# Values of a head and filling placed between the score steps of the wide attention heads

## The chip, the cores and the metric

The kernel runs on one core of a Trainium2 chip. A core has a matrix engine (TensorE, PE in the profile), VectorE (DVE), ScalarE (ACT), GpSimd (POOL) and SyncE (SP), which here only issues DMAs; they run side by side, each through its own list of instructions in order, and semaphores order them among one another. Matmuls read SBUF and write PSUM. The metric is the device time of one execution in microseconds, the median of three runs.

## The reference

One inference step of a decoder with two layers of width 1024, for a prompt of 1024 tokens and for 8 sample tokens, in f32. Layer 0 has four differential attention heads and four HGRN2 heads, layer 1 has eight forgetting-attention heads and four mLSTM heads. In each layer the heads' outputs go through an output projection with a residual, and then through a squared-ReLU MLP (1024 to 4096 to 1024) with a residual. The two kinds of attention at issue, cut to what matters:

```
# differential attention, per head: two causal softmaxes, one set of values (128 wide)
probs(q, k) = softmax(where(mask, q @ k.T * scale + bias, NEG))
o = (probs(q1, k1) - lam * probs(q2, k2)) @ v          # then an RMS norm per head

# forgetting attention, per head (64 wide)
s = q @ k.T * scale + fq[:, None] - fk[None, :]
o = softmax(where(mask, s, NEG)) @ v
```

## The kernel before

**Precision.** An f32 operand a is held as two parts, ah and al (a minus ah), both in a form that the matrix engine takes at full rate. A product then takes three matmuls: hi by hi, hi by lo, lo by hi. The parts of weights come from `wsplit` (L111 ff): a DMA brings 512 KB into wr (2 buffers), ScalarE copies them to wh (L117), GpSimd makes wl = wr - wh (L118).

**Stages.** The prompt is worked in two halves of 512 tokens, u = 0 and 1. The second half of attention is called wide, since its queries look back on up to 1024 keys: `diff_wide` (L746 ff, four heads, layer 0) and `fox_wide` (L1357 ff, eight heads, layer 1). A wide head has two groups, g = 2 and 3, each of two blocks of 128 queries. A query block has a score step: matmuls into S (L596 to L599; two PSUM buffers of 1024 columns), on VectorE a reduction for the row's extreme (L642, L644), on ScalarE the exponential e with its sum (L646), and then the scaling of e by the reciprocal sum (L769 to L772 in the differential heads, where a block has two score steps, m = 0 and 1; L1376 and L1380 in the forgetting heads). S is free again when its exponential is done.

Then a group is multiplied with the values in pairs of key blocks (3 pairs for g = 2, 4 for g = 3): `tr` transposes the probabilities of a pair on the matrix engine into pm (L664), ScalarE and VectorE split them into Ph and Pl (L652, L653), and `pv` multiplies them with the values' parts into po (L679). The values of a head are themselves transposed into pm and split: `diff_values` (transposes L702, Vh L704 on ScalarE, Vl L705 on VectorE) and `fox_values` (L1312, L1316, L1317; two heads in one pass, VV). pm is a single PSUM buffer, which these transposes share with those of the probabilities and with the sums of `head_norm` (hsq L294, hms L296, hrs L298 to L301, ho L303), the end of a differential head.

**Filling.** While a wide stage runs, the matrix engine is also given another half's output projection and MLP, the generator `half` (L1500 ff): parts of up to nine matmuls of 512 columns (L151), whose results VectorE adds to x (L1522), splits (xl L249, sq L261) or rectifies (L1495 to L1498). `tick(n)` adds n times a rate to a credit and takes parts from the generator until the credit is spent; a unit is 4096 columns, which is eight matmuls of 512. In both wide stages the rate is 1. What of the half is left when the stages end is drained without anything between.

**Order.** A tile scheduler sets the order of each engine's list from the program's order and its own timeline. In the wide stages the first matmul of every part of filling is tied (`issue_after`, L150) behind the last score, transpose or value product of the program so far, so that filling stays about where `tick` put it.

**The loop that the change touches** is `attend` (L602 ff). The groups of all heads form one list. A prologue prepares the first group, ticks 5, and does all its score steps, with tick(1.6) behind each. Then, group by group, a pair's transposes (`tr`), a tick and the next group's share of score steps, and the products (`pv`). A group marked late (only g = 2 in `diff_wide`) has its score steps held for the last two pairs of the group before. The values of head 0 are made inside `tr` of the first pair, so behind all score steps of the first group; those of later heads at the end of the head before's first group. `head_norm` of a differential head comes at the end of its group 3, next to the score steps of the next head.

Of the kernel before, what the change touches and what calls it, by code (L numbers as in the profile page):

```python
# [57 lines left out]
class Group:  # L58


    def __init__(self, prep, steps, pairs, tr, pv, end, late=False):
        self.prep, self.steps, self.pairs, self.tr, self.pv, self.end, self.late = prep, steps, pairs, tr, pv, end, late


class Step:
# [536 lines left out]
    def attend(self, groups, depth, lead, gap):  # L602

        self.chain = True
        N = len(groups)
        for G in groups[:depth + lead]:
            G.prep()
        self.tick(5)  # L610
        for G in groups[:depth]:
            for step in G.steps:
                step()
                self.tick(1.6)
        for n, G in enumerate(groups):
            if n + depth + lead < N:
                groups[n + depth + lead].prep()
            nxt = groups[n + depth] if n + depth < N else None
            todo = list(nxt.steps) if nxt else []
            for j in range(G.pairs):  # L620
                parts = G.tr(j)
                share = 0 if nxt and nxt.late and j < G.pairs - 2 else -(-len(todo) // (G.pairs - j if not (nxt and nxt.late) else min(2, G.pairs - j)))
                self.tick(max(gap - 0.4 * share, 0.4))
                for _ in range(share):
                    todo.pop(0)()
                G.pv(j, parts)
            G.end()
        self.chain = False
# [117 lines left out]
    def diff_wide(self, hd, pm, pS):  # L746
# [26 lines left out]
            P[h, i] = es[0]  # L773

        def tr(h, g, j):
            if h == j == 0 and g == 2:
                V[0] = self.diff_values(vt[0], u, hd, pm)
            if g == 2 and j == 0:
                po[h] = pm.tile([128, 512], F32, name="po", tag="po", bufs=1)
                if h < 3:  # L780
                    vt[h + 1] = self.values(self.O["va"][128 * h + 128:128 * h + 256, :], u, hd)
            return self.prob_t(hd, pm, (P[h, 2 * g], P[h, 2 * g + 1]), g, j)
# [16 lines left out]
        for h in range(4):  # L799
            for g in (2, 3):  # L800
                steps = [lambda h=h, i=i, m=m: score(h, i, m) for i in (2 * g, 2 * g + 1) for m in range(2)]
                groups.append(Group(lambda h=h, g=g: prep(h, g), steps, g + 1, lambda j, h=h, g=g: tr(h, g, j),
                                    lambda j, p, h=h, g=g: pv(h, g, j, p), lambda h=h, g=g: end(h, g), late=g == 2))
        self.attend(groups, 1, 0, 1.3)


# [550 lines left out]
    def fox_wide(self, hd, pm, pS):  # L1357
# [24 lines left out]

        def tr(h, g, j):
            i, r = divmod(h, 2)
            if h == j == 0 and g == 2:
                VV[0] = self.fox_values(vt[0], u, hd, pm)
            if g == 2 and j == 0:
                po[h] = pm.tile([128, 512], F32, name="po", tag="po", bufs=1)
                if r and i < 3:
                    vt[i + 1] = load(i + 1)  # L1390
            return self.prob_t(hd, pm, (P[h, 2 * g], P[h, 2 * g + 1]), g, j)
# [17 lines left out]
        for h in range(8):  # L1409
            for g in (2, 3):  # L1410
                groups.append(Group(lambda h=h, g=g: prep(h, g), [lambda h=h, qi=qi: score(h, qi) for qi in (2 * g, 2 * g + 1)], g + 1,
                                    lambda j, h=h, g=g: tr(h, g, j), lambda j, p, h=h, g=g: pv(h, g, j, p), lambda h=h, g=g: end(h, g)))
        self.attend(groups, 1, 1, 1.3)

    def fox_ones(self, W, hd):
# [489 lines left out]
```

## Time and profile before

| | |
|---|---|
| median of three runs | 2897.57 us (2889.6 to 2901.08) |
| the profiled execution | 2897.19 us |
| its span in the trace | 2895.4 us |
| mean granted clock of the matrix engine | 0.973 of full speed |
| PE busy | 2748.0 us, 95% |
| DVE / ACT / POOL busy | 48% / 36% / 39% |

The profile comes from one execution. "Busy" is time in which an instruction of the engine runs. The granted clock is the matrix engine's own, 1.00 at its full 2.4 GHz and 0.50 at its lower level of 1.2 GHz; a mean between the two is a mixture of both. A row of the timeline gives the start of an instruction from the span's start, its duration, the engine, the line of the kernel, what it writes and reads, how many are merged, and in brackets how long the engine had been idle and which instruction's end let it go on. Matmuls are pipelined: the distance of two starts, not the duration, is what one costs.

### The profile page before, as it was taken

What the parts mean: (1) busy time and instruction counts of PE and PEld (TensorE: products, weight loads), DVE (VectorE), ACT (ScalarE), POOL (GpSimd) and SP (SyncE); (2) the same over time, 40 slices, a digit from 0 to 9 for tenths busy, and PEclk for the clock granted to TensorE, in tenths of its full rate; (3) what the DMA queues carried; (4) which work ended last, traced back from release to release, by engine and by line L of the source; (5) the groups of instructions that cost most, each with busy time, mean ns of one, the idle gap of its engine ahead of it and who ended that gap; (6) DMA issues with size and microseconds to landing.
All of it is one profiled execution on the core that took longest, in us unless ns stands there. A gap on an engine that the chain in (4) does not pass through costs nothing. (4 is left out here: it accounts for less than half of the span.)

```text
span 2895.4 us, 44560 instructions
## 1 busy us (share of the span) xinstructions
PE 2748.0 (95%) x17404; PEld 2449.9 (85%) x17406; DVE 1377.6 (48%) x2666; ACT 1038.9 (36%) x1741; POOL 1142.3 (39%) x689
## 2 busy tenths in 40 slices
PE   8999997989989999999999989989999998999998
PEld 6999886777878878889999979968877776999997
DVE  5134378666664363474322255366544434523234
ACT  4111365552222232463232332155543222423233
POOL 2323323323764434423334435743323343344443
PEclk9999998999999999999999999999999998999999
DMA  4332454224545444423322244643235333322222
GB/s 143 107 125 75 152 163 127 89 83 154 159 115 164 132 163 147 154 88 104 121 95 88 91 158 147 222 128 93 77 110 163 110 107 126 110 89 95 90 94 74
DMA packets 174684, 349.72 MB, mean 121 GB/s; under 512 B 28914, under 2 KB 67298, under 8 KB 174474
## 3 DMA queue, kind: packets, MB, share of 16 engines
q1 hardware_dynamic: 174250, 346.81, 37.0%
q8 instruction: 137, 2.24, 0.3%
q0 software_dynamic: 224, 0.07, 0.2%
q14 instruction: 73, 0.60, 0.1%
HBM read 297.92 MB, written 48.88 MB: 120 GB/s over the span
## 5 line engine op out<-in xcount | busy, mean ns | idle before, releaser
L118 POOL TENSOR_TENSOR wl<-wr,wh 128x1024 fp32r<-128x1024 f32 (+1 forms) x361 | 866.2, 2400 | 1336.0 <-ACT wh L117 1293.1
L117 ACT ACTIVATE wh<-wr 128x1024 fp32r<-128x1024 f32 (+1 forms) x361 | 381.7, 1058 | 1088.1 <-PE acc L151 875.0
L151 PE MATMUL acc<-xh,wh 128*128 128x264 f32 (+2 forms) x2208 | 715.0, 325 | 18.1 <-DVE x L1522 8.0
L151 PE MATMUL acc<-xl,wh 128*128 128x264 f32 (+2 forms) x2208 | 711.3, 323 | 3.1 <-DVE xl L249 3.1
L151 PE MATMUL acc<-xh,wl 128*128 128x264 f32 (+2 forms) x2208 | 709.9, 322 | 0.0
L151 PE MATMUL acc<-uh,wh 128*128 128x512 f32 (+2 forms) x1856 | 607.4, 331 | 21.7 <-DVE x L1522 13.2
L151 PE MATMUL acc<-ul,wh 128*128 128x512 f32 (+2 forms) x1856 | 599.6, 324 | 6.9 <-DVE ul L1489 5.6
L151 PE MATMUL acc<-uh,wl 128*128 128x512 f32 (+2 forms) x1856 | 597.6, 323 | 0.0
L151 PEld LDWEIGHTS acc<-xh,wh 128*128 128x128 f32 x2208 | 420.3, 191 | 51.5 <-issue 10.5
L151 PEld LDWEIGHTS acc<-xl,wh 128*128 128x128 f32 x2208 | 420.7, 191 | 35.6 <-DVE xl L249 4.3
L151 PEld LDWEIGHTS acc<-xh,wl 128*128 128x128 f32 x2208 | 420.0, 190 | 29.4 <-issue 1.2
L1522 DVE TENSOR_TENSOR x<-acc,x 128x256 f32<-128x256 f32 (+1 forms) x464 | 238.3, 517 | 379.0 <-PE acc L151 376.9
L151 PEld LDWEIGHTS acc<-uh,wh 128*128 128x128 f32 x1856 | 353.0, 192 | 56.7 <-DVE x L1522 17.0
L151 PEld LDWEIGHTS acc<-ul,wh 128*128 128x128 f32 x1856 | 354.2, 191 | 33.6 <-DVE ul L1489 7.6
L151 PEld LDWEIGHTS acc<-uh,wl 128*128 128x128 f32 x1856 | 353.8, 191 | 26.8 <-issue 0.4
L1495 DVE SCALAR_TENSOR_TENSOR acc<-acc,rb 128x256 f32<-128x256 f32 (+2 forms) x192 | 100.2, 524 | 242.4 <-PE acc L151 237.7
L151 PE MATMUL acc<-ih,wh 128*128 128x512 f32 (+3 forms) x600 | 193.0, 322 | 7.3 <-ACT wh L117 4.7
L151 PE MATMUL acc<-ih,wl 128*128 128x512 f32 (+3 forms) x600 | 192.2, 323 | 6.5 <-POOL wl L118 6.5
L151 PE MATMUL acc<-il,wh 128*128 128x512 f32 (+3 forms) x600 | 192.2, 321 | 0.0
L225 DVE TENSOR_TENSOR z<-acc,rb 128x512 f32<-128x512 f32 (+2 forms) x138 | 69.6, 511 | 231.2 <-PE acc L151 216.6
L1498 DVE TENSOR_TENSOR ul<-acc,uh 128x256 fp32r<-128x256 f32 (+2 forms) x192 | 98.5, 513 | 135.6 <-ACT uh L1497 134.9
L151 PEld LDWEIGHTS acc<-ih,wh 128*128 128x128 f32 (+1 forms) x600 | 113.8, 190 | 16.8 <-ACT wh L117 6.7
(409 smaller groups left out, 3406.1 us busy)
## 6 DMA issues: line engine op xcount, KB each, us to landing
wr<-in_w_up SPq DMA_DIRECT2D x128, 512.0 KB
wr<-in_w_down SPq DMA_DIRECT2D x128, 512.0 KB
wr<-in_w_in_o SPq DMA_DIRECT2D x48, 512.0 KB
wr<-in_w_out SPq DMA_DIRECT2D x32, 512.0 KB
wr<-in_w_in_e SPq DMA_DIRECT2D x27, 512.0 KB
qd<-qS SPq DMA_DIRECT2D x64, 128.0 KB
dk<-in_cache_k_a SPq DMA_DIRECT2D x32, 256.0 KB
dk<-in_cache_v_a SPq DMA_DIRECT2D x32, 256.0 KB
```

The source lines that it names most:

```text
L117: nc.scalar.activation(h[:, :kk, :m], r[:, :kk, :m], AF.Copy)
L118: nc.gpsimd.tensor_tensor(l[:, :kk, :m], r[:, :kk, :m], raw(h[:, :kk, :m]), op=ALU.subtract)
L151: nc.tensor.matmul(out, lhsT=w[:, k, :m], rhs=a[:, sl], start=(n == 0), stop=(n == last))
L225: nc.vector.tensor_tensor(d, p, r, op=ALU.mult)
L1495: nc.vector.scalar_tensor_tensor(p, p, 0.0, self.rb[u][:, sl], op0=ALU.max, op1=ALU.mult)
L1498: nc.vector.tensor_tensor(L[:, sl], p, raw(H[:, sl]), op=ALU.subtract)
L1522: nc.vector.tensor_tensor(x[f][:, sl], pt[:, :m], x[f][:, sl], op=ALU.add)
```

## The change

Two things are moved; the instructions themselves stay the same, on every engine. `attend` calls a group's new function `values` behind the first score step of the prologue, and `tr` no longer does it. And where the next group is late, the tick ahead of a pair's score steps is not lowered for them, and a tick(1) stands between one score step and the next. That holds for heads 1 to 3 of `diff_wide`; no group of `fox_wide` is late.

```diff
--- before.py
+++ after.py
@@ -58,8 +58,8 @@
 class Group:
 
 
-    def __init__(self, prep, steps, pairs, tr, pv, end, late=False):
-        self.prep, self.steps, self.pairs, self.tr, self.pv, self.end, self.late = prep, steps, pairs, tr, pv, end, late
+    def __init__(self, prep, steps, pairs, tr, pv, end, late=False, values=None):
+        self.prep, self.steps, self.pairs, self.tr, self.pv, self.end, self.late, self.values = prep, steps, pairs, tr, pv, end, late, values
 
 
 class Step:
@@ -609,9 +609,11 @@
             G.prep()
         self.tick(5)
         for G in groups[:depth]:
-            for step in G.steps:
+            for n, step in enumerate(G.steps):
                 step()
                 self.tick(1.6)
+                if n == 0 and G is groups[0]:
+                    G.values()
         for n, G in enumerate(groups):
             if n + depth + lead < N:
                 groups[n + depth + lead].prep()
@@ -620,9 +622,12 @@
             for j in range(G.pairs):
                 parts = G.tr(j)
                 share = 0 if nxt and nxt.late and j < G.pairs - 2 else -(-len(todo) // (G.pairs - j if not (nxt and nxt.late) else min(2, G.pairs - j)))
-                self.tick(max(gap - 0.4 * share, 0.4))
-                for _ in range(share):
+                late = share and nxt.late
+                self.tick(gap if late else max(gap - 0.4 * share, 0.4))
+                for i in range(share):
                     todo.pop(0)()
+                    if late and i < share - 1:
+                        self.tick(1)
                 G.pv(j, parts)
             G.end()
         self.chain = False
@@ -773,8 +778,6 @@
             P[h, i] = es[0]
 
         def tr(h, g, j):
-            if h == j == 0 and g == 2:
-                V[0] = self.diff_values(vt[0], u, hd, pm)
             if g == 2 and j == 0:
                 po[h] = pm.tile([128, 512], F32, name="po", tag="po", bufs=1)
                 if h < 3:
@@ -800,7 +803,8 @@
             for g in (2, 3):
                 steps = [lambda h=h, i=i, m=m: score(h, i, m) for i in (2 * g, 2 * g + 1) for m in range(2)]
                 groups.append(Group(lambda h=h, g=g: prep(h, g), steps, g + 1, lambda j, h=h, g=g: tr(h, g, j),
-                                    lambda j, p, h=h, g=g: pv(h, g, j, p), lambda h=h, g=g: end(h, g), late=g == 2))
+                                    lambda j, p, h=h, g=g: pv(h, g, j, p), lambda h=h, g=g: end(h, g), late=g == 2,
+                                    values=lambda: V.update({0: self.diff_values(vt[0], u, hd, pm)})))
         self.attend(groups, 1, 0, 1.3)
 
 
@@ -1382,8 +1386,6 @@
 
         def tr(h, g, j):
             i, r = divmod(h, 2)
-            if h == j == 0 and g == 2:
-                VV[0] = self.fox_values(vt[0], u, hd, pm)
             if g == 2 and j == 0:
                 po[h] = pm.tile([128, 512], F32, name="po", tag="po", bufs=1)
                 if r and i < 3:
@@ -1409,7 +1411,8 @@
         for h in range(8):
             for g in (2, 3):
                 groups.append(Group(lambda h=h, g=g: prep(h, g), [lambda h=h, qi=qi: score(h, qi) for qi in (2 * g, 2 * g + 1)], g + 1,
-                                    lambda j, h=h, g=g: tr(h, g, j), lambda j, p, h=h, g=g: pv(h, g, j, p), lambda h=h, g=g: end(h, g)))
+                                    lambda j, h=h, g=g: tr(h, g, j), lambda j, p, h=h, g=g: pv(h, g, j, p), lambda h=h, g=g: end(h, g),
+                                    values=lambda: VV.update({0: self.fox_values(vt[0], u, hd, pm)})))
         self.attend(groups, 1, 1, 1.3)
 
     def fox_ones(self, W, hd):
```

The matrix engine's list at the start of `diff_wide`, before: K_4648 and K_4651 are the parts of the first map's keys, K_4661 and K_4664 those of the second map's; hms is the last norm of the stage before, vt the values of head 0.

```order
L296 MATMUL hms<-hsq,ones 128x512
L596 MATMUL S<-K_4648,Q_4647 128x512
L599 MATMUL S<-K_4651,Q_4647 128x512
L596 MATMUL S<-K_4648,Q_4647 128x128
L599 MATMUL S<-K_4651,Q_4647 128x128
L596 MATMUL S<-K_4661,Q_4660 128x512
L599 MATMUL S<-K_4664,Q_4660 128x512
L596 MATMUL S<-K_4661,Q_4660 128x128
L599 MATMUL S<-K_4664,Q_4660 128x128
L702 MATMUL pm<-ident,vt 128x128 x4
```

And with the change, from the same place on:

```order
L296 MATMUL hms<-hsq,ones 128x512
L596 MATMUL S<-K_4648,Q_4647 128x512
L599 MATMUL S<-K_4651,Q_4647 128x512
L596 MATMUL S<-K_4648,Q_4647 128x128
L599 MATMUL S<-K_4651,Q_4647 128x128
L707 MATMUL pm<-ident,vt 128x128 x4
L596 MATMUL S<-K_4661,Q_4660 128x512
L599 MATMUL S<-K_4664,Q_4660 128x512
L596 MATMUL S<-K_4661,Q_4660 128x128
L599 MATMUL S<-K_4664,Q_4660 128x128
L596 MATMUL S<-K_4648,Q_4647 128x512
```

The values' first four transposes stood behind two score steps and now stand behind one; the second four move ahead of the first two filling matmuls.

The matrix engine's list at the turn from head 0 to head 1 in `diff_wide`, before: K_5555 and K_5568 with their partners are head 1's keys, hms is head 0's norm, e its probabilities.

```order
L596 MATMUL S<-K_5555,Q_5554 128x128
L599 MATMUL S<-K_5558,Q_5554 128x128
L296 MATMUL hms<-hsq,ones 128x512
L596 MATMUL S<-K_5568,Q_5567 128x512
L599 MATMUL S<-K_5571,Q_5567 128x512
L596 MATMUL S<-K_5568,Q_5567 128x128
L599 MATMUL S<-K_5571,Q_5567 128x128
L596 MATMUL S<-K_5555,Q_5554 128x512
L599 MATMUL S<-K_5558,Q_5554 128x512
L596 MATMUL S<-K_5555,Q_5554 128x256
L599 MATMUL S<-K_5558,Q_5554 128x256
L664 MATMUL pm<-ident,e 128x128 x4
```

With the change (there K_5609 and K_5612 are the second map's keys of head 1), from the end of the filling inside the second score on; twelve more filling rows stand ahead of these, and three where lines are left out:

```order
L151 MATMUL acc<-ul,wh 128x512
L151 MATMUL acc<-uh,wl 128x512
L599 MATMUL S<-K_5612,Q_5608 128x512
L596 MATMUL S<-K_5609,Q_5608 128x128
L599 MATMUL S<-K_5612,Q_5608 128x128
L151 MATMUL acc<-uh,wh 128x512
L151 MATMUL acc<-ul,wh 128x512
L151 MATMUL acc<-uh,wl 128x512
...
L669 MATMUL pm<-ident,e 128x128 x4
L151 MATMUL acc<-uh,wh 128x512
```

Before, no filling stood between the scores of both maps, the norm's sums and the transposes; now 14 filling matmuls stand in the second score, 6 behind it, and 6 more behind the transposes, ahead of the third score. The sums of the last wide norm come 87 instructions later on this engine than before.

VectorE's list near the start of `fox_wide`, before: VV_19299 and VV_19300 are the split values of heads 0 and 1 (each in two pieces), e the scaled probabilities, xl, sq and x belong to the filling.

```order
L1380 TENSOR_SCALAR e<-e,st 128x768
L1522 TENSOR_TENSOR x_16979<-acc,x_16979 128x512
L1376 RECIPROCAL st<-st 128x1
L1317 TENSOR_TENSOR VV_19299<-pm,VV_19299 128x4x64
L1380 TENSOR_SCALAR e<-e,st 128x896
L249 SCALAR_TENSOR_TENSOR xl_19318<-x_16979,col,xh_19317 128x512
L1522 TENSOR_TENSOR x_16995<-acc,x_16995 128x512
L261 TENSOR_TENSOR sq<-sq,sqt 128x512
L1317 TENSOR_TENSOR VV_19300<-pm,VV_19300 128x4x64
L642 TENSOR_REDUCE st<-S 128x1
```

With the change, where VV_19251 and VV_19252 are the same values:

```order
L1321 TENSOR_TENSOR VV_19251<-pm,VV_19251 128x4x64
L1384 TENSOR_SCALAR e<-e,st 128x768
L1525 TENSOR_TENSOR x_16979<-acc,x_16979 128x512
L1380 RECIPROCAL st<-st 128x1
L1321 TENSOR_TENSOR VV_19252<-pm,VV_19252 128x4x64
L1384 TENSOR_SCALAR e<-e,st 128x896
L1525 TENSOR_TENSOR x_16995<-acc,x_16995 128x512
L249 SCALAR_TENSOR_TENSOR xl_19300<-x_16979,col,xh_19299 128x512
L261 TENSOR_TENSOR sq<-sq,sqt 128x512
L647 TENSOR_REDUCE st<-S 128x1
```

The second pieces of both values stood behind the scalings of 768 and 896 columns, an xl and an sq; now one is ahead of each scaling. The reduction at the end of the rows has not moved.

## Rows read from the trace of the kernel before

**Rows 1.** The page: busy time, share of the span, instructions.
```profile
PE 2748.0 (95%) x17404; PEld 2449.9 (85%) x17406; DVE 1377.6 (48%) x2666; ACT 1038.9 (36%) x1741; POOL 1142.3 (39%) x689
```

**Rows 2.** Windows: busy us of each engine, then granted clock, DMA share, GB/s.
```profile
core 0: us, PE busy (x) PEld busy (x) DVE busy (x) ACT busy (x) POOL busy (x), PEclk, DMA share, GB/s
440.00:670.00 230.00, 197.83 (x957) 163.79 (x956) 156.48 (x275) 125.61 (x202) 69.24 (x29) 0.92 0.29 91
478.00:499.00 21.00, 11.81 (x50) 9.25 (x50) 20.91 (x28) 13.90 (x22) 10.40 (x4) 0.85 0.43 131
548.00:558.00 10.00, 8.93 (x34) 7.76 (x35) 5.17 (x11) 1.58 (x5) 0.00 (x0) 0.52 0.08 30
594.00:600.00 6.00, 5.01 (x21) 4.43 (x22) 4.37 (x10) 2.26 (x4) 0.00 (x0) 0.72 0.11 44
637.00:644.00 7.00, 5.46 (x23) 4.71 (x24) 2.94 (x5) 2.42 (x5) 0.00 (x0) 0.76 0.92 321
800.00:820.00 20.00, 12.03 (x57) 9.52 (x56) 19.01 (x18) 2.12 (x2) 14.41 (x12) 0.84 0.41 120
880.00:960.00 80.00, 80.00 (x375) 66.08 (x375) 38.87 (x89) 23.14 (x30) 33.53 (x17) 1.00 0.50 158
```

**Rows 3.** Waits of PE, 440 to 670 us: total, times, longest.
```profile
PE S L596 <- ACT e L646: 11.9, 6, 3.6
PE po L679 <- DVE Pl L653: 6.9, 3, 5.3
PE pm L664 <- DVE hrs L301: 2.7, 1, 2.7
```

**Rows 4.** Timeline of PE, turn from head 0 to head 1.
```profile
548.39 0.80 PE L596 MATMUL S<-K,Q 128*128 128x512 f32 x1 [3.63 <-ACT e L646]
...
554.30 0.63 PE L151 MATMUL acc<-ul,wh 128*128 128x512 f32 x1
554.73 0.63 PE L151 MATMUL acc<-uh,wl 128*128 128x512 f32 x1
...
559.60 0.39 PE L151 MATMUL acc<-ul,wh 128*128 128x512 f32 x1
559.83 0.40 PE L151 MATMUL acc<-uh,wl 128*128 128x512 f32 x1
```

**Rows 5.** Timeline of PE, the next two turns.
```profile
594.99 0.75 PE L596 MATMUL S<-K,Q 128*128 128x512 f32 x1 [3.38 <-ACT e L646]
...
637.86 0.66 PE L664 MATMUL pm<-ident,e 128*128 128x128 f32 x4 [2.69 <-DVE hrs L301]
```

**Rows 6.** Timeline of POOL and DVE, first head.
```profile
473.14 2.41 POOL L118 TENSOR_TENSOR wl<-wr,wh 128x1024 fp32r<-128x1024 f32 x1 [6.78 <-ACT wh L117]
...
473.40 2.96 DVE L772 SCALAR_TENSOR_TENSOR e<-e,rl 128x768 f32<-128x768 f32 x1
...
488.48 1.14 DVE L772 SCALAR_TENSOR_TENSOR e<-e,rl 128x896 f32<-128x896 f32 x1
```

**Rows 7.** Timeline of PE at the start of `diff_wide`.
```profile
452.67 0.66 PE L702 MATMUL pm<-ident,vt 128*128 128x128 f32 x4 [0.91 <-DVE hrs L301]
455.55 0.79 PE L596 MATMUL S<-K,Q 128*128 128x512 f32 x1 [2.22 <-ACT e L646]
```

**Rows 8.** Timeline of DVE and PE near the start of `fox_wide`.
```profile
1911.29 2.24 DVE L1380 TENSOR_SCALAR e<-e,st 128x896 f32<-128x896 f32 x1
...
1914.72 2.25 DVE L261 TENSOR_TENSOR sq<-sq,sqt 128x512 f32<-128x512 f32 x1
...
1917.22 1.21 DVE L642 TENSOR_REDUCE st<-S 128x1 f32<-128x1024 f32 x1
...
1917.45 1.09 PE L664 MATMUL pm<-ident,e 128*128 128x128 f32 x4 [6.28 <-DVE VV L1317]
```

**Rows 9.** Timeline of DVE and PE in the HGRN stage behind.
```profile
804.29 10.30 DVE L404 TENSOR_TENSOR hq<-hq,hpe 128x256 f32<-128x256 f32 x1
...
817.34 0.77 PE L151 MATMUL acc<-xh,wh 128*128 128x512 f32 x1 [7.38 <-DVE x L1522]
```

## The prediction

> **What bounds the kernel now.** I read the page first. TensorE (PE) is busy 2748.0 of 2895.4 us [rows 1], so the other engines count only where they make PE wait, and the most that can be won anywhere is PE's idle time and what a low clock costs it. The change acts in two stretches, so I asked for the windows next. In the wide differential stage, 440 to 670 us, PE is busy 197.83 of 230 us at a mean granted clock of 0.92; VectorE (DVE) is full there for a time (20.91 of 21 us), and in the stretches around 553, 597 and 640 us the clock is 0.52, 0.72 and 0.76 [rows 2]. In the drain of filling at 880 to 960 us PE is busy 80.00 of 80 us at clock 1.00 [rows 2]: matmuls taken from there shorten it one for one, and they are a gain to the extent that they come to stand in idle time. The list of waits then says who is late in 440:670: score matmuls wait six times for the exponential that frees one of the two S buffers (11.9 us), the value product three times for Pl (6.9), and a probability transpose once for the head norm's hrs, which reads the single pm buffer (2.7) [rows 3]. Last I read the timeline at those places.
>
> **Filling between the score steps.** At a late group (g = 2 of heads 1 to 3, while group 3 of the head before is multiplied) tick(0.5) becomes tick(1.3) before a pair of score steps, and tick(1) comes between the two. That is 0.8 + 1 = 1.8 units in each of two pairs of three heads, 10.8 units of 4096 columns, or 86 matmuls of 512 columns. The instruction orders agree: PE's position at the last wide head's hms is 87 later, while the whole list of PE's instructions holds the same ones. At full clock two successive filling matmuls start 0.23 us apart, at the low clock 0.43 [rows 4]; 87 x 0.23 = 20 us of filling comes ahead. It costs nothing by itself, since the drain ends that much earlier. So the gain is the idle time that it covers plus the clock that it saves.
>
> At the turn from head 0 to head 1 the next score waits 3.63 us for the exponential [rows 4]. In the changed order 14 and 6 filling matmuls stand in the second score, and 6 behind the transposes: 26 x 0.23 = 6.0 us of work where PE idled 3.63. At the next two turns the waits are 3.38 us (for the exponential) and 2.69 us (for hrs) [rows 5], with 16 and more matmuls in front in the changed order. Together 9.7 us. What is late next is hsq, Q's low part or a busy DVE, all of them now nearer behind the score: I leave 0.5 us for each turn, so 8.2 us go. Of the 11.9 us of waits for the exponential, 11.9 - 3.63 - 3.38 - 2.22 (the entry, below) = 2.7 us are small ones at other places of the same turns; I take half, 1.3.
>
> The clock: behind these waits PE is busy 8.93 us at 0.52, 5.01 us at 0.72 and 5.46 us at 0.76 [rows 2]. At full clock that is 8.93 x 0.48 + 5.01 x 0.28 + 5.46 x 0.24 = 4.3 + 1.4 + 1.3 = 7.0 us less. The row of 548.39 shows how it comes: PE idles 3.63 us, and from there its matmuls run at half pace for some 9 us [rows 2, 4]. With the long gaps filled I count 5.5 of the 7.0. The page "TensorE: Matmul & The Clock Gate" of the Trainium skill, section "HAM oscillation — how this bites in real kernels", says the same of pauses in front of short bursts, and by it shorter gaps could still bring the low clock if they recur; then the term would be 2 to 3 us and the forecast about 2883.
>
> What it costs: 87 matmuls need some 3 more weight blocks inside the stage (by the code a block serves 24 to 32 matmuls), each with a load of 512 KB on SP's queue, a wh on ScalarE and a wl on GpSimd (POOL) of 2.41 us [rows 6], in front of the next head's loads on SP and its K low part on POOL. DMA moves at a share of 0.29 of its engines here [rows 2], so I cost the loads at nothing; if the head's loads do come late, the new trace shows scores that wait for Q's low part, which is not among the longest waits now [rows 3]. The wl blocks are another matter. The scaling of 896 columns of e took 1.14 us with POOL idle, the one of 768 columns took 2.96 us while a wl ran from 473.14 [rows 6]. From these rows each meeting costs DVE about 2 us. Three wl more, each met with a chance of a half, are 3 us where DVE is full, and I charge them to PE; the bounds are 0 (all meet idle time) and 6.
>
> The page "SBUF — State Buffer" of the Trainium skill, section "Who interferes with whom", gives the reason and speaks against this change: a VectorE instruction with two inputs in SBUF and a GpSimd instruction that reads SBUF exclude each other for a whole instruction, and whoever issues second waits. Rows 6 agree. By that rule alone every new wl could cost its whole 2.4 us, 7 us in all, and the forecast would be 2884.
>
> **Values behind the first score.** Each of the two wide stages moves 8 transposes on PE, with their copies Vh or VV on ScalarE, their low parts on DVE and two ticks of 1.3, ahead of the remaining score steps of the first group. No DMA moves: vt was loaded in prep before as well. At the entry of the differential stage the first four transposes waited for hrs until 452.67, because pm has one buffer, and the third score waited 2.22 us for the exponential at 455.55 [rows 7]. Now the second score stands behind the transposes and starts some 2 us later; but DVE, which works on the head norm's output then, reaches its reduction only little later. Vl gets ahead of the second reduction, and what follows no longer finds it in the way. I put this at 1 us gained. From 462 to 503 us DVE is full and sets the pace, and it has the same work; it begins about 1 us earlier, and PE no longer stands for Pl at the end of it for all of 5.3 us (the largest part of the 6.9 in rows 3), as filling is shifted there. I put it at 2.3 us. Bounds for both: a gain of 7 (the 2.22 and most of the Pl wait go) and a loss of 4 (the later second score is passed on through the full DVE).
>
> In the forgetting stage PE waits 6.28 us at 1917.45 for VV to leave pm, and VV stood on DVE behind the scaling of 896 columns (2.24 us) and sq (2.25 us) [rows 8]. Now its last part stands ahead of both, so the transposes can start about 5 us earlier. But the score behind them needs the buffer of the 1024-column score, whose reduction still comes at 1917.22 [rows 8] on a DVE that does the same work. So most of the 6.28 us becomes a wait at that score, with 6 more filling matmuls done before it (6 x 0.23 = 1.4 us), and somewhat less of it at low clock. I take 2 us gained; bounds 5 (the whole wait, less what is passed on) and a loss of 2.
>
> **Later.** The filling shifts by 20 us against the stages behind. In one of them POOL is busy 14.41 of 20 us, DVE's hq takes 10.30 us, and PE waits 7.38 us [rows 9, 2]. Whether such a meeting stays, goes or doubles depends on instants I can't see; I take 0, with 11 either way: 7.38 us and some 3.8 us of low clock (0.84 in 800:820 over 12.03 us is 1.9, and as much again behind it, an estimate).
>
> **The sum** against the profiled execution (2897.19 us, span 2895.4; the median of the runs, 2897.57, is the same within 0.4): -8.2 - 1.3 - 5.5 + 3 - 1 - 2.3 - 2 + 0 = -17.3 us, so 2880 us.
>
> **Rivals.** First, the waits only move. For it: DVE has 20.91 of 21 us of work in one stretch [rows 2], and what PE waits for at each place is the end of a chain that ends on DVE or behind it. Against it: DVE is idle a third of the whole stage, and at the turns the chain is a latency. Then only a third of the 9.5 us of score waits goes, half of the 7.0 us of clock, and nothing at either entry: -3.2 - 3.5 + 3 = -4, or 2893 us.
>
> Second, slower: the filling moved by 20 us makes POOL and DVE meet as at 804.29, where one two-input instruction of DVE stood still through a row of POOL's [rows 9]. Each costs 11 us as above. It decides from the second new one on: two cost 22 us, while the wide stage yields half (about -9), so +13 or 2910 us. For it: the work of POOL that it needs (sample products, wl) is there from 670 us on. Against it: in the stage itself POOL is busy a third of the time, and PE's idle time in the whole span is only 2895.4 - 2748.0 = 147 us [rows 1].
>
> Third, more: the same shift takes the one meeting at 804.29 away. Then 11 us come on top, 2869 us.
>
> Fourth, the values moved ahead hold the second score back through pm, and the entry loses its 4 us instead of gaining 3.3: 2887 us. It is an end of the range of the forecast.
>
> **How the numbers follow.** Forecast, with the fourth in it: 0.50. Waits only move: 0.28. More: 0.12. Slower: 0.10. About 0.5%, 14.5 us, is what can be told from no change here. The forecast's own range is 2872 to 2888: its unknown terms (clock 3, blocks 3, entries 4 and 3) rarely go one way together. Two thirds of it lie beyond 2883, 0.33 of 0.50; of the waits that only move nearly nothing, 0.03; all of the third: faster 0.48. Slower by 14.5 us is half of the second rival and a little more for what I don't see: 0.08. The rest, 0.44, is the same. The range from 2863 to 2900 leaves out the upper part of the second rival and the extremes of the third.
>
> **What would show it.** Right: in the stage between 440 and 670 us (shorter in the new trace, or holding some 87 filling matmuls more) the waits for the exponential fall from 11.9 to below 5 us, the clock behind the first turn stays above 0.9, and the drain behind the HGRN stage holds 60 to 90 matmuls fewer at full clock. At the forgetting entry VV's wait is gone and a score waits for an exponential for 3 to 5 us. Wrong: if PE's idle time in the stage stays near 32 us with other names, if wl rows stand beside DVE instructions of 2 to 10 us at new places, or if the drain is shorter by 20 us and yet the span is not.

## The result and the profile after

The changed kernel takes 2871.28 us (median of 6 runs, 2869.53 to 2875.49) against 2896.31 us for the kernel before, timed beside it. The ratio is 0.9923 with a 95% interval of 0.9905 to 0.9941, so 22 us less (17 to 28); the two medians lie 25 us apart. The forecast was 17 us less, 2880 us. The result lies inside the stated range of 2863 to 2900, 9 us below the forecast and just below the 2872 to 2888 that the forecast was given without its rivals. The profiled execution took 2873.62 us, with a span of 2871.9.

Most of it is won where it was looked for. The windows of the kernel before first, cut at the head norms (the stretch up to head 0's norm, then the three turns, and all four together; columns as in [rows 2]):

```profile
449.40:543.00 93.60, 76.22 (x351) 62.35 (x350) 72.76 (x123) 57.22 (x94) 29.31 (x13) 0.89 0.28 85
543.00:588.70 45.70, 40.33 (x197) 33.72 (x196) 32.56 (x58) 24.85 (x40) 13.38 (x6) 0.89 0.28 86
588.70:634.00 45.30, 39.26 (x201) 32.73 (x200) 30.22 (x54) 25.34 (x43) 10.95 (x5) 0.96 0.13 48
634.00:666.50 32.50, 29.12 (x152) 24.50 (x151) 14.77 (x32) 12.51 (x19) 7.20 (x3) 0.95 0.38 133
449.40:666.50 217.10, 184.93 (x896) 153.30 (x895) 150.31 (x266) 119.93 (x194) 60.83 (x25) 0.91 0.26 85
```

And of the changed kernel, between the same norms:

```profile
450.20:541.80 91.60, 79.06 (x356) 65.18 (x354) 67.76 (x124) 57.10 (x94) 28.60 (x13) 0.87 0.30 87
541.80:590.70 48.90, 47.24 (x244) 39.32 (x245) 35.48 (x62) 28.43 (x46) 19.29 (x8) 1.00 0.37 106
590.70:636.60 45.90, 43.60 (x230) 36.59 (x229) 30.55 (x60) 26.59 (x45) 12.60 (x6) 1.00 0.21 65
636.60:669.00 32.40, 30.28 (x158) 25.49 (x157) 14.71 (x31) 13.38 (x20) 9.15 (x4) 0.95 0.37 123
450.20:669.00 218.80, 200.19 (x982) 166.58 (x981) 148.50 (x273) 125.49 (x202) 69.63 (x29) 0.94 0.31 92
```

The stage is no shorter, 218.8 against 217.1 us, but it holds 86 more matmuls on PE (982 against 896). To compare, I take off 0.228 us, the distance of two filling matmuls at full clock, for each of the 4, 50, 26 and 7 filling matmuls that the order shifts into the four stretches:

| stretch | before | after | filling moved in | after, filling counted | difference |
|---|---|---|---|---|---|
| to norm of head 0 | 93.6 | 91.6 | 0.9 | 90.7 | -2.9 |
| head 0 to 1 | 45.7 | 48.9 | 11.4 | 37.5 | -8.2 |
| head 1 to 2 | 45.3 | 45.9 | 5.9 | 40.0 | -5.3 |
| head 2 to 3 | 32.5 | 32.4 | 1.6 | 30.8 | -1.7 |
| the stage | 217.1 | 218.8 | 19.8 | 199.0 | -18.1 |
| from there until VectorE reads the next projection's sums (HGRN stage and drain) | 385.4 | 361.7 | -19.8 | 381.5 | -3.9 |

The rest of the 23.5 us between the two traces lies outside these stretches: the stage starts 0.8 us later, and the stages behind differ by -4.1 to +5.0 us and by 2.3 us less in sum. What made these later differences is not shown; two traces of the unchanged kernel differ there by at most 1.5 us in a stage.

PE's timeline at the first turn, the answer to [rows 4]: no wait is left, and no low clock.

```profile
542.85 0.50 PE L596 MATMUL S<-K,Q 128*128 128x512 f32 x1
543.19 0.40 PE L151 MATMUL acc<-ul,wh 128*128 128x512 f32 x1
...
546.18 0.40 PE L151 MATMUL acc<-uh,wl 128*128 128x512 f32 x1
546.41 0.39 PE L599 MATMUL S<-K,Q 128*128 128x512 f32 x1
...
548.25 0.60 PE L669 MATMUL pm<-ident,e 128*128 128x128 f32 x4
...
550.07 0.40 PE L596 MATMUL S<-K,Q 128*128 128x512 f32 x1
```

At the next two turns, the answers to [rows 5], 1.43 and 2.12 us are left of 3.38 and 2.69:

```profile
595.72 0.50 PE L596 MATMUL S<-K,Q 128*128 128x512 f32 x1 [1.43 <-ACT e L651]
...
639.81 0.66 PE L669 MATMUL pm<-ident,e 128*128 128x128 f32 x4 [2.12 <-DVE hrs L301]
```

In the first head, the answer to [rows 7], the two waits have only shared out their time differently (1.59 + 1.53 us against 0.91 + 2.22), and in place of the 5.3 us for Pl [rows 3] stand a wait for a scaled e and one for an exponential:

```profile
453.42 0.66 PE L707 MATMUL pm<-ident,vt 128*128 128x128 f32 x4 [1.59 <-DVE hrs L301]
...
456.24 0.80 PE L596 MATMUL S<-K,Q 128*128 128x512 f32 x1 [1.53 <-ACT e L651]
...
479.79 0.74 PE L669 MATMUL pm<-ident,e 128*128 128x128 f32 x3 [2.75 <-DVE e L777]
...
495.44 0.79 PE L596 MATMUL S<-K,Q 128*128 128x512 f32 x1 [3.83 <-ACT e L651]
```

PE's waits in 440 to 660 us, the answer to [rows 3]: total, times, longest.

```profile
PE S L596 <- ACT e L651: 7.3, 4, 3.8
PE pm L669 <- DVE e L777: 2.7, 1, 2.7
PE pm L669 <- DVE hrs L301: 2.1, 1, 2.1
PE po L684 <- DVE Pl L658: 1.8, 2, 1.7
PE pm L707 <- DVE hrs L301: 1.6, 1, 1.6
```

Of the 7.3 us for the exponential 5.4 lie in the first head (the rows of 456.24 and 495.44).

At the forgetting entry, the answer to [rows 8], VV is early, and the wait has become one of a score for the exponential behind the same late reduction, as forecast:

```profile
1885.38 0.40 DVE L1321 TENSOR_TENSOR VV<-pm,VV 128x256 fp32r<-128x256 f32 x1
...
1891.64 1.21 DVE L647 TENSOR_REDUCE st<-S 128x1 f32<-128x1024 f32 x1
...
1894.14 0.79 PE L596 MATMUL S<-K,Q 128*128 128x512 f32 x1 [3.08 <-ACT e L651]
```

### The profile page after: what moved, and what is told of

Same layout as the page of the kernel before. It is cut to its first block, busy times and chain, and to the rows that moved or that the text cites. A ratio compares the mean times of both kernels' runs of the same rounds, so it can differ in the third digit from the quotient of the medians.

```text
span 2871.9 us, 44542 instructions
## 1 busy us (share of the span) xinstructions
PE 2741.4 (95%) x17405; PEld 2444.9 (85%) x17406; DVE 1356.8 (47%) x2666; ACT 1036.5 (36%) x1741; POOL 1145.2 (40%) x689
```

## The experiments

All were timed beside the kernel before. "Ahead" is the number of filling matmuls ahead of the last wide norm beyond those of before. The last three columns are read from each run's trace, with 0.228 us per matmul counted, as in the table above; "three turns" is the wide stage from head 0's norm on. A trace shows one execution, whose time stands in front of them, and that is not always near the median: those of e1_values, e9_light_start and e10_values_gap are the fastest of their runs, that of e5_gap is the slowest, and e6_between's lies 10 us above its median.

| run | ahead | median us | ratio to before (95%) | traced run us | three turns | wide stage | HGRN stage and drain |
|---|---|---|---|---|---|---|---|
| before | 0 | 2897.57 | 1 | 2897.19 | 123.5 | 217.1 | 385.4 |
| e0_before_again | 0 | 2893.08 (one run) | | 2893.08 | 123.7 | 217.3 | 383.7 |
| the change | 87 | 2871.28 | 0.9923 (0.9905 to 0.9941) | 2873.62 | 108.3 | 199.0 | 381.5 |
| e1_values | 0 | 2890.75 | 0.9980 (0.9961 to 0.9998) | 2883.82 | 121.9 | 215.0 | 374.7 |
| e2_filling | 87 | 2877.55 | 0.9931 (0.9907 to 0.9955) | 2880.52 | 109.3 | 204.6 | 382.2 |
| e4_in_front | 87 | 2874.92 | 0.9929 (0.9907 to 0.9951) | 2874.92 | 108.3 | 202.1 | 376.8 |
| e7_not_fox | 87 | 2871.07 | 0.9919 (0.9897 to 0.9941) | 2871.97 | 108.4 | 201.7 | 378.6 |
| e5_gap | 35 | 2880.78 | 0.9956 (0.9937 to 0.9974) | 2888.32 | 110.3 | 202.7 | 384.3 |
| e10_values_gap | 35 | 2880.06 | 0.9952 (0.9932 to 0.9971) | 2873.45 | 110.2 | 200.7 | 384.2 |
| e6_between | 48 | 2889.25 | 0.9983 (0.9964 to 1.0001) | 2899.06 | 113.5 | 209.6 | 385.6 |
| e8_more | 130 | 2878.95 | 0.9953 (0.9932 to 0.9975) | 2883.29 | 108.1 | 199.6 | 390.0 |
| e9_light_start | 63 | 2886.16 | 0.9975 (0.9960 to 0.9990) | 2878.42 | 112.3 | 204.5 | 383.7 |
| e3_bulk | 0 (87 behind) | 2891.11 | 0.9992 (0.9974 to 1.0010) | 2891.04 | 123.5 | 217.2 | 380.5 |
| e11_gap_bulk | 35 (52 behind) | 2874.38 | 0.9940 (0.9920 to 0.9960) | 2875.08 | 112.2 | 202.6 | 382.7 |

### Each part alone

e1_values is the change without its second part:

```diff
-                self.tick(gap if late else max(gap - 0.4 * share, 0.4))
+                self.tick(max(gap - 0.4 * share, 0.4))
...
-                    if late and i < share - 1:
-                        self.tick(1)
```

> Only the first part of the change: the values of head 0 behind the first score step in both wide stages, the ticks as before. My theory (the gain is waits and low clock covered by filling at the three turns): 1 to 4 us less than before, all of it at the two entries, with the 11.9 us of waits for the exponential at the turns unchanged; about 2893 us. Rival (the values carry the gain, by freeing VectorE and pm early): 12 us or more of the 25 come already here, about 2884 or below. Second rival (the second score is held back): slower than before by 2 to 4 us.

It is 6 us faster (0.5 to 11), above my 1 to 4, which the interval holds, and below the rival's 12. In the stage it gains 2.1 us, only 0.5 of them in the first head, and the turns keep their waits, as in [rows 4, 5]. PE's timeline at the first two turns:

```profile
546.30 0.50 PE L596 MATMUL S<-K,Q 128*128 128x512 f32 x1 [3.64 <-ACT e L648]
...
590.43 0.79 PE L596 MATMUL S<-K,Q 128*128 128x512 f32 x1 [3.38 <-ACT e L648]
```

The other 1.6 us stand in the turns, where the granted clock is 0.96 in the first in place of 0.89 and 0.93 in the second in place of 0.96; why is not shown. The traced run is 7 us faster than the median, and its HGRN stage 10.7 us shorter than before; how much of that the other runs have is not shown.

e2_filling is the kernel before with only the second part, and e4_in_front the same with the tick(1) moved ahead of the pair:

```diff
-                self.tick(gap if late else max(gap - 0.4 * share, 0.4))
+                self.tick(gap + 1 if late else max(gap - 0.4 * share, 0.4))
...
-                    if late and i < share - 1:
-                        self.tick(1)
```

> Only the second part: filling between the score steps of the late groups, values where they were. My theory: 18 to 24 us less than before (2872 to 2878), with the clock of the first two turns back at 1.00 and the waits for the exponential below 8 us in the differential stage; the forgetting entry keeps its wait of about 6 us for VV. Rival (the values carry the gain): less than 12 us.

> As the run with filling only, but the tick(1) stands ahead of a pair's two score steps instead of between them (2.3 units ahead, none between), so that the amount is the same. My theory (the wait that is covered is the second step's wait for the exponential of the S buffer, so it matters that filling stands between): half of the turn's gain goes, the waits for the exponential stay above 9 us, 10 to 14 us less than before, about 2885 us. Rival (the amount alone pays, since any filling ahead gives VectorE and ScalarE time to catch up): within 4 us of the run with filling only.

Filling alone gives 20 us (13 to 27) of the 22, so the rival in which the values carry the gain falls. What the values add beside it, 6 us by the medians, lies within the overlap of the two intervals. The second comparison fell out otherwise than I had expected, and it decides nothing: the lists of e2_filling and e4_in_front are the same on PE but for a handful of rows, the 14 filling matmuls inside head 1's second score included. The scheduler had put them there although the program issues them ahead. The two runs are thus a repeat of one another, and they tell how far two traces of nearly the same order differ: 2.5 us in the wide stage and 5.4 in the HGRN stage.

### The two ticks apart, and more

e5_gap keeps only the undiminished tick ahead, e6_between only the tick(1) between; e10_values_gap is e5_gap with the values moved, and e8_more the change with a larger tick between:

```diff
-                        self.tick(1)
+                        self.tick(2)
```

> Only the undiminished tick(1.3) ahead of the late pairs, no tick(1) and the values where they were: 35 filling matmuls come ahead of the last wide norm instead of 87. If gain goes with the amount: 35/87 of the 20 us of the run with filling only, 8 us less than before, about 2888 us. Rival (saturation: each covered wait is under 4 us, which 16 matmuls fill, so that a part of the filling does nearly all): 15 us or more less, 2881 us or below. Second rival (a third score still waits for its exponential, with the low clock behind it): within 4 us of before.

> Only the tick(1) between the score steps of a late pair, the tick ahead lowered as before, the values where they were: 48 filling matmuls ahead of the last wide norm. If gain goes with the amount: 48/87 of 20 us, 11 us less than before, about 2885 us. Rival (saturation): 16 us or more less, 2880 us or below. Second rival (the first score's wait stays open): within 5 us of before.

> The changed kernel without the tick(1) between the score steps: values behind the first score, and the undiminished tick ahead of late pairs. My theory after the runs so far (the ahead tick covers nearly all that filling can cover at the turns, tick(1) adds nothing that can be measured, and the values add about 5 us in the differential stage): within 5 us of the changed kernel, 2867 to 2877 us, the wide stage 18 us shorter than before with its filling counted. Rival (tick(1) is needed beside the values): 8 us or more slower than the changed kernel.

> The changed kernel with tick(2) instead of tick(1) between the steps: 130 filling matmuls ahead of the last wide norm instead of 87. My theory (what can be covered is covered; of the 18.6 us that the matrix engine still idles in the stage some 11 lie in the first head, where VectorE is full): within 4 us of the changed kernel, 2868 to 2874 us. Rival (gain goes with the amount): 43 matmuls at 0.21 us each, 9 us less than the changed kernel, about 2862 us. Second rival (more weight blocks meet VectorE): 4 us or more slower than the changed kernel.

In the wide stage, 35 matmuls by the tick ahead gain 14.4 us, 48 by the tick between 7.5, 87 by both 12.5 and 15.0; with the values, 35 gain 16.4, 87 gain 18.1 and 15.4 (e7_not_fox), 130 gain 17.5. The three turns alone, where the filling stands, tell it with less scatter: 35 gain 11 to 13 us in three traces (e5, e10, e11), 48 between 10, 87 by both 14 to 15 in four (the change, e2, e4, e7), and 130 also 15. The gain does not go with the amount, and it saturates: the tick ahead covers most of what can be covered, and the tick between adds 1 to 4 us to it. It adds them in the second turn, where e10_values_gap keeps a wait of 2.83 us for the exponential and a clock of 0.92, against 1.43 us and 1.00 in the change; in the third turn it is the change that keeps a wait, 2.12 us. In e5_gap's trace the 3.63 us wait of the first turn has become 0.82 us, with the clock of that turn at 1.00. Its window first:

```profile
540.60:584.40 43.80, 42.03 (x223) 35.29 (x222) 33.43 (x62) 26.85 (x43) 17.49 (x7) 1.00 0.36 109
```

And the row of its timeline on PE:

```profile
547.08 0.50 PE L596 MATMUL S<-K,Q 128*128 128x512 f32 x1 [0.82 <-ACT e L647]
```

The whole time says more than that, though. e8_more is 8 us slower than the change, which of my expectations only the second rival had, and e10_values_gap 9 us slower (their intervals and that of the change overlap). Both have the change's wide stage within 2 us. For e10_values_gap no trace shows the loss: its traced run, at 2873.45 us, is as fast as the change's. What the record does show is the granted clock of every run, over its whole span: 0.969 to 0.974 in the ten of e10_values_gap, 0.974 to 0.976 in the six of the change, and at 0.974 the two take 2873.45 and 2875.49 us. The same holds inside one kernel: of the runs of the kernel before beside e10_values_gap, the fastest, 2886.79 us, had 0.975 and the slowest, 2908.92 us, 0.968. So the loss goes with a lower clock in most of its runs; where in them, and why, is not shown. e8_more's traced run is 10 us slower than the change's, and 8.5 us of that lie in the HGRN stage. VectorE's hq stands for 10.29 us there, and PE waits, as in [rows 9]. The timeline of VectorE there:

```profile
817.46 10.29 DVE L404 TENSOR_TENSOR hq<-hq,hpe 128x256 f32<-128x256 f32 x1
```

And of PE:

```profile
830.50 0.77 PE L151 MATMUL acc<-uh,wh 128*128 128x512 f32 x1 [7.37 <-DVE x L1525]
```

### Where the filling meets the stage behind

e0_before_again is the kernel before, unchanged. e3_bulk has the amount and not the place:

```diff
         self.attend(groups, 1, 0, 1.3)
+        self.tick(10.8)
```

> The kernel before, unchanged, profiled once more, to see whether the 10.30 us of VectorE's hq at 804.29 us and the 7.38 us wait behind it belong to its order or to one execution. If to one execution (my theory after the runs so far, since none of the five other traces has them, the one with the same filling order included): no VectorE instruction above 4 us between 700 and 900 us, and the stretch from the last wide norm to the first sums of the next projection is 374 to 381 us instead of 385.4. Rival (it belongs to the order): again about 10 us at the same instruction, 385 us.

> The kernel before with a single tick(10.8) behind the last wide differential head: as many filling matmuls are ahead of the HGRN stage as with the change, but none of them between score steps. My theory (where filling stands is what pays, and only about 7 us come from the shift of filling against the HGRN stage): the wide stage's waits stay near 32 us, 4 to 8 us less in all, about 2891 us. Rival (the shift of filling against the HGRN stage is the main gain): 18 us or more less, 2879 us or below. Second rival (the shift is worth nothing): within 3 us of before.

The unchanged kernel's second trace has no such hq, so the 10.30 us of [rows 9] are not fixed by the order. VectorE's timeline there:

```profile
807.06 1.35 DVE L404 TENSOR_TENSOR hq<-hq,hpe 128x256 f32<-128x256 f32 x1
```

Of fourteen traces three have it, of kernels with 0, 48 and 130 matmuls ahead; none of the six with 87 ahead at the first HGRN norm (e3_bulk and e11_gap_bulk among them) has it, nor have five of the other eight. But its absence was worth only 1.7 us in that stretch, since other waits took its place, 3.32 us at 816.82 for a weight block among them. e3_bulk keeps the whole of the wide stage's waits (217.2 us), and it is between 8 us faster and 3 us slower than before: the shift alone is not the gain. That rival falls; whether the shift gives a few us or nothing this run cannot tell.

e11_gap_bulk is e10_values_gap with tick(6.5) in the same place, so that 52 more matmuls stand behind the wide stage and the filling meets the HGRN stage as it does in the change.

> The run with the values and the undiminished tick (35 matmuls ahead, 2880.06 us), with one tick(6.5) behind the last wide differential head: 87 filling matmuls are then ahead at the first HGRN norm, as with the changed kernel, but the 52 that tick(1) would put between score steps stand in one piece behind the stage. My theory now (tick(1) gains nothing inside the wide stage, where both kernels need the same time with filling counted; its 8 us come behind it, from how the filling meets the HGRN stage's small matmuls and their clock): equal to the changed kernel within 4 us, about 2872 us, with the HGRN stretch 376 to 382 us with its filling counted, and its clock near 0.98. Rival (tick(1) pays where it stands): as the run without it, 2878 to 2882 us, the HGRN stretch at 384 us with its filling counted.

2874.38 us lies 3 us above the change and 6 us below e10_values_gap, so the median is nearer to my theory. But its interval covers both, and its trace has 382.7 us in the HGRN stage at a clock of 0.96, which I had given to neither. The medians put tick(1) at 3 us (e2_filling against e5_gap) and 9 us (the change against e10_values_gap), with intervals that overlap both times; 1 to 4 us of that stand in the three turns, against my theory, and the rest stays open.

### The forgetting stage, and the first head

e7_not_fox is the change with the forgetting heads' values back inside tr; e9_light_start has less filling in the first differential head:

```diff
-                self.tick(1.6)
+                self.tick(0.8 if G.late else 1.6)
```

> The changed kernel with the values of the forgetting stage made where they were before. In the engines' lists only one group of four transposes and the low parts behind it move. My theory (the values in the forgetting stage bring 2 to 4 us at its entry at most): 0 to 4 us slower than the changed kernel, 2871 to 2876 us, with VectorE's VV late again and a wait of 2 to 6 us at the entry. Rival (this part is what lifts the result from the 2877 us of filling alone): 6 us or more slower than the changed kernel.

> The changed kernel with tick(0.8) instead of tick(1.6) behind the score steps of the first differential head, where VectorE is full: less filling, and with it less of VectorE's x, xl and sq, in the first head; 63 instead of 87 matmuls ahead of the last wide norm. If VectorE's work sets the pace of the first head: its stretch from the last norm before it to its own norm gets 3 to 6 us shorter with its filling counted, 2866 to 2870 us in all. Rival (the chain of reductions, exponentials and transposes sets it, not VectorE's load): no shorter, 0 to 5 us slower in all than the changed kernel, since filling that covered waits is gone.

Without the forgetting part the time is the same, 2871.07 us, although its trace has a wait for VV back (6.28 us before):

```profile
1890.79 0.63 PE L669 MATMUL pm<-ident,e 128*128 128x128 f32 x4 [4.78 <-DVE VV L1321]
```

The stretch from the sums ahead of the layer's projections to the sums behind this entry takes 225.9 us in that trace and 226.9 in the changed kernel's. The wait was a latency, behind which the same reduction came last.

e9_light_start was slower than the change by 15 us, more than either expectation had. Its first stretch is 90.9 us against 91.6, with 10 matmuls (2.3 us) fewer in it, so no shorter with its filling counted. But VectorE was busy 70.62 us in it, with 123 instructions, against 67.76 with 124: the run did not take load off VectorE there, so whether that load sets the first head's pace stays open. Some 3 to 5 us of the loss lie in the wide stage (204.5 us against 199.0 and 201.7), 4 of them in the turns, where 69 matmuls stand in place of 83. Its traced run, the fastest of twelve, is only 5 us slower than the change's, so no trace shows the rest.

## Why the prediction was right, and where it was not

**The filling at the turns** was the main term: 8.2 + 1.3 us of waits and 5.5 of clock, less 3 for weight blocks, 12.0 us. With both ticks the three turns gained 14.2 to 15.2 us in four traces, two of them without the values moved. The mechanism is shown where the wait was longest: in the first turn the wait and the low clock of [rows 2, 4] go when filling stands there (e2_filling, e5_gap), and the wait stays when it does not (e1_values, e3_bulk). In the changed kernel PE's idle time in the turns fell by 8.7 us (9.5 forecast) and its busy time, with filling counted, by 6.5 (5.5 forecast for the clock). The second turn kept the full clock although a wait of 1.43 us is left in it, so the forecast's alternative of 2 to 3 us for the clock did not come in this trace; e2_filling's, with the same order there, has 0.96. The three long waits gave less than their 8.2 us, since 1.43 and 2.12 are left, and small ones more than 1.3; that the sum fits is luck in part.

What failed in the term is its last part. The 3 us for weight blocks that meet VectorE did not come: between the norms of heads 0 and 1 GpSimd is busy 19.29 us in place of 13.38, VectorE 35.48 in place of 32.56 with four instructions more, and PE idles 1.7 us in place of 5.4. There VectorE has slack. One of the two rows behind the price of 2 us a meeting was read too simply: in the trace GpSimd starts a K at 489.20, inside the scaling at 488.48, so GpSimd was idle only when the scaling was issued, and here it was GpSimd's instruction that took longer (2.67 us for 2.41). The rule of the Trainium skill's page "SBUF — State Buffer" (section "Who interferes with whom"), that a VectorE instruction with two inputs in SBUF and a GpSimd instruction that reads SBUF exclude each other, agrees with the 2.85 us row below; but in these turns the meetings cost PE nothing that the traces show.

**The entry of the differential stage** was put at 3.3 us, and the first stretch gained 2.9. That the size fits is luck: the steps were not those of the forecast, and e7_not_fox, with the change's own order up to the forgetting stage, gained 0.3 there. Neither the entry waits nor the wait for Pl shrank in sum: 5.3 us for Pl became 2.75 + 3.83 for others, as in e1_values (3.67 + 3.85). What went are a wait of 2.85 us for the filling's x and smaller ones. VectorE's busy time in that stretch shrank from 72.76 to 67.76 us with all but the same instructions (123 and 124). With the values moved it is 67.8 to 70.6 us in seven traces (the change, e1 and e7 to e11), without them 71.1 to 72.8 in the other seven. PE's idle time there goes with it: 12.0 to 15.0 us in the seven with the values moved, 16.7 to 17.8 in the others. But the seven also have a granted clock of 0.86 to 0.87, where five of the others have 0.89, and with its filling counted PE is busy 1.9 us longer in the changed kernel; why the clock is lower is not shown. The same kinds of instruction are still drawn out when GpSimd runs, as here, though fewer of them: four take over 1.9 us in the changed kernel's stretch, seven before. GpSimd's row in the changed kernel's timeline:

```profile
474.78 2.41 POOL L577 TENSOR_TENSOR K<-kd,K 128x1024 fp32r<-128x1024 f32 x1 [1.64 <-ACT K L573]
```

And VectorE's, issued 0.1 us later:

```profile
474.89 2.85 DVE L261 TENSOR_TENSOR sq<-sq,sqt 128x512 f32<-128x512 f32 x1
```

So the new order happens to let fewer two-input instructions meet GpSimd's. That is a reading of the sums; no run moved one such meeting by itself.

**The forgetting stage** was put at 2 us and is worth nothing that can be measured (e7_not_fox). The wait moved as forecast; what failed is the step from there to a gain, the 1.4 us of filling ahead of the score that were counted as won.

**Later** was put at 0, with 11 either way. The traces give 3.9 us less for the change; over the six traces with the same shift the stretch takes 376.8 to 382.7 us, against 383.7 and 385.4 before, so 1 to 9 us less. That the shift is the cause is not shown: e1_values, without any, has 374.7 us. Of the 9 us between forecast and result 3 are the blocks' term and some 4 this one, less 2 for the forgetting stage; the rest is the spread of the runs, which for the kernel before go from 2885 to 2910 us. That the terms missed in both directions and the sum came near is luck in part. Of the rivals, "the waits only move" was right for the waits named at both entries and wrong for the turns. "More" was right in its sign and in that the stall of 804.29 is gone, but the second trace of the kernel before shows that the absence of the stall earns 2 us and not 11. "Slower" needed two such stalls; e8_more has one and is 8 us behind the change. The fourth, that the values hold the second score back, falls with e1_values, whose first stretch is 0.5 us shorter than before and not 4 longer.

Of what the trace was to show, the clock of the first turn (1.00), the forgetting entry (3.08 us) and the shorter drain came. The waits for the exponential fell to 7.3 us and not below 5, because 5.4 of them are the first head's.

## What to carry to other kernels

Where one engine does the work and waits for short chains on others, look for the few places where a chain is waited for with nothing else queued, and put independent work there in the amount of the wait: here 35 matmuls at the turns gained most of what 130 did. Work that is only moved costs nothing here, since the place it leaves is full; but it shifts everything behind, and the stage behind took from 374.7 to 390.0 us over these traces, for reasons that they do not show, so compare stage by stage with the moved work counted, and see whether the traced run lies near the median that it is to explain. And read the list that the scheduler makes: two programs that differed in where filling is issued had the same one.

## What the runs showed of the hardware that was not expected

A VectorE instruction with two inputs stood through a whole row of GpSimd instructions, not through one, and the same instruction of the same kernel did not do so in the next trace. In the kernel before, hq was issued at 804.29 and ended when GpSimd's row without a pause ended (its last row here starts at 811.84 and takes 2.47 us). GpSimd's timeline:

```profile
803.91 3.77 POOL L863 TENSOR_TENSOR dk<-dk,dq 128x512 f32<-128x512 f32 x3
807.63 2.39 POOL L118 TENSOR_TENSOR wl<-wr,wh 128x1024 fp32r<-128x1024 f32 x1
809.98 1.27 POOL L863 TENSOR_TENSOR dk<-dk,dq 128x512 f32<-128x512 f32 x1
811.22 0.66 POOL L405 TENSOR_TENSOR hk<-hk,hpe 128x256 f32<-128x256 f32 x1
811.84 2.47 POOL L863 TENSOR_TENSOR dk<-dk,dq 128x512 f32<-128x512 f32 x2
```

In the changed kernel GpSimd ran just as closely, and hq came through at the change from one of its instructions to the next. GpSimd's rows:

```profile
806.26 2.37 POOL L118 TENSOR_TENSOR wl<-wr,wh 128x1024 fp32r<-128x1024 f32 x1
808.56 5.15 POOL L867 TENSOR_TENSOR dk<-dk,dq 128x512 f32<-128x512 f32 x4
```

VectorE's row:

```profile
807.54 1.37 DVE L404 TENSOR_TENSOR hq<-hq,hpe 128x256 f32<-128x256 f32 x1
```

What decides between the two was not tried.
